# Row sums of squares of the next superblock's x, moved from the end of a superblock into its second merge

## The chip, the cores and the metric

The kernel runs on one core of a Trainium2 chip. The metric is the device time of one execution in microseconds; before the change three runs gave a median of 2172.32 us (2170.7 to 2173.43). PE, DVE, ACT, POOL and SP are the core's engines (matmul, vector, scalar, GpSimd, and the queue that issues most transfers). Each of them works through its instructions in the order in which they are laid out.

## What is computed

One layer over 2048 tokens of width 1024, in f32, with three branches that read the same normalised input `h`:

```
def rms_norm(x, g):
    y = xf * lax.rsqrt(jnp.mean(xf * xf, axis=-1, keepdims=True) + RMS_EPS)
    return (y * g.astype(jnp.float32)).astype(x.dtype)
...
h = rms_norm(x, norm_g[l])
p = h @ w_in[l]
...
y_a = rwkv7_mix(p_r, p_k, p_v, p_w, p_a, ...) * jax.nn.silu(z_a)
y_b = sliding_window_sink_attn(p_q, p_sk, p_sv, positions, ...) * jax.nn.silu(z_b)
y_c = memory_cross_attn(p_xq, mem, ...) * jax.nn.silu(z_c)
merged = (gates[:, :, 0] * (y_a @ w_proj_a[l]) + gates[:, :, 1] * (y_b @ w_proj_b[l])
          + gates[:, :, 2] * (y_c @ w_proj_c[l]))
x = x + (merged.astype(x.dtype) @ w_out[l]).astype(x.dtype)
```

The change concerns the mean of `xf * xf` over a token's 1024 values, of which `rms_norm` needs the inverse root.

## The kernel before

**Tiling.** The tokens are worked in four superblocks, 0 to 3, of 512 tokens. A projection is eight k-blocks of 128; each f32 operand is split into two parts (`hH`/`hL`, `yh`/`yl`, the two halves of `whl`), and three matmuls 128x512 (L505 to L507) make one k-block, so a merge step is 4 x 3 = 12 matmuls and a projection 24. Weights come in blocks through six `whl` buffers: in superblock 0 SP loads `raw`, ACT (L487) and DVE (L488) split it, and the parts are stored to DRAM; later superblocks load the parts ready made. Matmuls of projections and merges write two PSUM banks `mm` in turn; a bank is free again when its reader is done.

**A superblock.** Two streams of work are interleaved. One is the recurrent branch: preparation, an inverse by 31 dependent DVE steps on `Yi` and `ibc` (L863 to L865), its transpose (L868), 64 small matmuls that read it (L880), then the chain over chunks. The other is cross-attention, window attention in four pairs of heads (`swa_pair`, whose end L1253, `split_y` L1032 on ACT and L1033 on DVE makes a `yh`/`yl` tile), beside which runs the merge of branch c, then the merge of branch b (called the second merge here: eight steps, each with its gate projection, tanh L1261, and L1276/L1277), then the eight gates of branch a. After both streams come the rope tables (L566 to L587, with two sines on ACT that need another activation table), `x_scales` for the next superblock, the merge of branch a (third merge: L1276 empties a bank, L1277 adds, L1281 and L1283 split the sum), `x_cols` and `output`.

**x_scales and x_cols.** For the next 512 tokens, eight tiles 128x512 of x are loaded by transfers that ACT issues (L1318) into the ring `rt` of six buffers; ACT squares each (L1320) into a bf16 tile that nobody reads, of the ring `ibc` that the inverse uses too, and sums along the row by `accum_out`. DVE adds the two halves of a row (L1322), POOL takes the power -1/2 (L465, L467), DVE spreads the 512 scales (L543), four PE transposes (L545) turn them along the tokens, ACT copies them from PSUM (L1327). `x_cols` then loads eight tiles of transposed x (L1336), scales each (L1339) and splits it into `hH` and `hL` (L1341, L1342).

**What sets the order.** All instructions are collected in the order in which the program writes them, and a list scheduler (`lay_out`) with a table of costs lays out one order for each engine. It takes what is ready, by rank (the place in the program), and opens tiles of a ring in program order. A transfer is planned by it to land some 2.2 us after its issue plus its bytes. The ring `g2` has 11 buffers for the attention tiles, the gates and the output's tiles. Transfers report their landing on eight semaphores in turn, each of which is used again only when the transfer before on it has landed.

Of the kernel before, what the change touches and what calls it, by code (L numbers as in the profile page):

```python
# [9 lines left out]
F32 = mybir.dt.float32  # L10
F32R = mybir.dt.float32r
BF16 = mybir.dt.bfloat16
I32 = mybir.dt.int32
U8 = mybir.dt.uint8
AF = mybir.ActivationFunctionType
ALU = mybir.AluOpType
# [3 lines left out]
T, D, M = 2048, 1024, 256  # L20
TB = 512
# [12 lines left out]
EPS = 1e-6  # L34
# [282 lines left out]
def build(tc, A, nsb=4):  # L317
    nc = tc.nc
    es = ExitStack()
    V, S, G, PE = nc.vector, nc.scalar, nc.gpsimd, nc.tensor  # L320

    def pool(name, bufs, **kw):
        return es.enter_context(tc.tile_pool(name=name, bufs=bufs, **kw))
# [5 lines left out]
    rp = pool("rp", 1)  # L329
# [5 lines left out]
    xp = pool("xp", 1)  # L335

    def g2(dt=F32, shape=(128, TB)):
        return gp_.tile(list(shape), dt, name="g2")
# [3 lines left out]
    def mm_ps():  # L342
        return ps.tile([128, 512], F32, name="mm", bufs=2)
# [4 lines left out]
    def s_ps():  # L348
        return ps.tile([128, 512], F32, name="as_", bufs=2)
# [34 lines left out]
    memt, mem0, raws, x0, xt0 = [], [], [], [], []  # L384
# [75 lines left out]
    def rpow(out, in_, add, scale=1.0):  # L460

        if scale == 1.0:
            G.tensor_scalar(out, in_, add, None, op0=ALU.add)  # L463
        else:
            G.tensor_scalar(out, in_, scale, add, op0=ALU.mult, op1=ALU.add)  # L465
        n = out.shape[-1]
        G.tensor_tensor(out, out, mhalf[:, :n], op=ALU.pow)  # L467
# [12 lines left out]
    def wblock(src, key=None):  # L480
        w = wp.tile([128, 2, 512], F32R, name="whl")
        if key in kept:
            nc.sync.dma_start(w.bitcast(F32), kept[key])
            return w[:, 0], w[:, 1]
        raw = wp.tile([128, 512], F32, name="raw", bufs=RAW)
        nc.sync.dma_start(raw, src)
        S.activation(w[:, 0], raw, AF.Copy)  # L487
        V.tensor_tensor(w[:, 1], raw, w[:, 0].bitcast(F32), op=ALU.subtract)  # L488
        if key is not None and nsb > 1:
            kept[key] = dp.tile([128, 2, 512], F32, name=f"k{len(kept)}")  # L490
            nc.sync.dma_start(kept[key], w.bitcast(F32))
        return w[:, 0], w[:, 1]
# [8 lines left out]
    def gemm3(out, pairs):  # L501

        n = len(pairs)
        for i, ((lh, ll), (rh, rl)) in enumerate(pairs):
            PE.matmul(out, lh, rh, start=i == 0, stop=False)  # L505
            PE.matmul(out, lh, rl, start=False, stop=False)  # L506
            PE.matmul(out, ll, rh, start=False, stop=i == n - 1)  # L507
# [107 lines left out]
    def row_sums(rows):  # L615

        ss = xp.tile([128, 4, 2], F32, name="ss", bufs=2)
        for i, xr in enumerate(rows):
            sq = rp.tile([128, 512], BF16, name="ibc", bufs=2)
            if i % 2:  # L620
                V.tensor_tensor_reduce(sq, xr, xr, 1.0, 0.0, ALU.mult, ALU.add, ss[:, i // 2, 1:])
            else:
                S.activation(sq, xr, AF.Square, accum_out=ss[:, i // 2, :1])
        rs = xp.tile([128, 4], F32, name="rs", bufs=2)
        n = len(rows) // 2
        V.tensor_tensor(rs[:, :n], ss[:, :n, 0], ss[:, :n, 1], op=ALU.add)
        return rs
# [89 lines left out]
    def tmp(tag="rt", bufs=NRT):  # L717
        return rp.tile([128, TB], F32, name=tag, bufs=bufs)
# [539 lines left out]
    def gate(i, o, hT):  # L1258
        gp = proj(B_G + 8 * i + o, hT)
        t = gp_.tile([128, TB], F32, name="gt", bufs=2) if i else g2()  # L1260
        S.activation(t, gp, AF.Tanh, scale=0.5)  # L1261
        return t

    def merge(i, yh, yl, accs, hT, first=False, orange=range(8), gates=None):
        for o in orange:
            yield 3.718
            w = [t.rearrange("p (k c) -> p k c", k=4) for t in wblock(A["w_proj"][i, o], ("proj", i, o))]
            g = gates[o] if gates else gate(i, o, hT)
            pp = mm_ps()
            gemm3(pp, [((w[0][:, k], w[1][:, k]), (yh[k], yl[k])) for k in range(4)])  # L1270
            if first:
                acc = mp.tile([128, TB], F32, name="mB")
                V.scalar_tensor_tensor(acc, g, 1.0, pp, op0=ALU.add, op1=ALU.mult)
                accs.append(acc)
            else:
                V.scalar_tensor_tensor(g, g, 1.0, pp, op0=ALU.add, op1=ALU.mult)  # L1276
                V.tensor_tensor(accs[o], accs[o], g, op=ALU.add)  # L1277
# [25 lines left out]
    def masks():  # L1303
        full = g2()[:, :384]
        nc.sync.dma_start(full, A["gmask"])
        for i, t in enumerate((gmask, upto, over)):
            G.tensor_copy(t, full[:, i * 128:(i + 1) * 128])

    def x_scales(sb):

        if not sb:
            rs = row_sums(x0)
        else:
            ss = xp.tile([128, 4, 2], F32, name="ss", bufs=2)
            for i in range(4):
                for u in range(2):
                    xr = tmp()
                    nc.scalar.dma_start(xr, A["x"][sb * TB + i * 128:sb * TB + (i + 1) * 128, u * 512:(u + 1) * 512])  # L1318
                    sq = rp.tile([128, 512], BF16, name="ibc", bufs=2)
                    S.activation(sq, xr, AF.Square, accum_out=ss[:, i, u:u + 1])  # L1320
            rs = xp.tile([128, 4], F32, name="rs", bufs=2)
            V.tensor_tensor(rs, ss[:, :, 0], ss[:, :, 1], op=ALU.add)  # L1322
        rpow(rs, rs, EPS, 1.0 / D)
        bc = s_ps()
        bcast_T(bc, rs, 1, 4)
        rb = tmp()
        S.activation(rb, bc, AF.Copy)  # L1327
        return rb
# [19 lines left out]
    mv(3)  # L1348
    for i, _ in enumerate(mem_kv(mT, ms, mr)):
        if i == AT1:  # L1350
            rb = x_scales(0)
        if i == AT2:
            masks()
            hT = x_cols(0, rb)
    for sb in range(nsb):
        wa = proj(B_WA, hT)
        low = shift(wa, B_WA, pcol("mu_wa"), dcol("omu_wa"), sb, "rr_")
        S.activation(low[EV], low[EV], AF.Tanh)

        lwla = [rp.tile([128, TB], F32R, name=f"lwla{i}") for i in range(2)]  # L1360
        for t, h, o in zip(lwla, (EV, OD), (OD, EV)):
            S.activation(t[h], low[h], AF.Copy)
            V.tensor_tensor(t[o], low[h], t[h].bitcast(F32), op=ALU.subtract)
        yas = []
        ya, yb, yc_ = ([], []), ([], []), ([], [])
        accs = []

        def stream_r():
            parks = park(sb)
            dk = xp.tile([128, 4, NC_], F32, name="dk", bufs=1)  # L1370
            Pl = xp.tile([128, 4, NC_], F32, name="Pl", bufs=1)
            yts = []
            for p0 in (0, 2):
                group = []
                Nc = rp.tile([128, 2, NC_, 32], F32, name="Nc")
                for p in (p0, p0 + 1):
                    yield from rwkv_prep(p, p - p0, parks, dk, Pl, Nc, sb, hT, lwla, group)
                yield from rwkv_inverse(group, parks, Nc)
                yts += [g[2] for g in group]
            yield from rwkv_chain(parks, dk, Pl, hT, yts, yas)  # L1380
            yield 0.412

        def stream_f():
            for h in range(4):
                yield from cross_head(h, sb, hT, *yc_)
            if not sb:
                rope_tables(0)
            yield from swa_kv(sb, hT)
            yield 6.938
            for j in range(4):  # L1390
                yield from weave(swa_pair(j, sb, hT, *yb), merge(2, *yc_, accs, hT, first=True, orange=(2 * j, 2 * j + 1)))
            yield from merge(1, *yb, accs, hT)
            for o in range(8):
                gates.append(gate(0, o, hT))
                yield 5.908

        gates = []
        for _ in weave(*(paced(g, PACE[min(sb, 1)][i]) for i, g in enumerate((stream_r(), stream_f())))):
            pass
        for p in range(4):  # L1400
            split_y(yas[p], *ya, "a", p, sb)
        rb = None
        if sb + 1 < nsb:
            rope_tables(sb + 1)
            rb = x_scales(sb + 1)
        parts = []
        for o in range(8):
            for _ in merge(0, *ya, accs, hT, gates=gates, orange=(o,)):
                pass
            parts.append(split_acc(accs[o]))  # L1410
        if rb is not None:
            hT = x_cols(sb + 1, rb)
        output(sb, *zip(*parts))
# [92 lines left out]
```

## Time and profile before

| | us |
|---|---|
| median of three runs | 2172.32 |
| lowest, highest | 2170.7, 2173.43 |
| the profiled execution | 2170.66 |
| its span | 2168.9 |

A timeline row reads: start, duration, engine, line, operation, output<-input, shape, count, and in brackets how long the engine had been idle and what released it. Rows with a letter q behind the engine (ACTq) are that engine's queue issuing a transfer; that is not counted as busy time. Waits are listed as: who waited, for whom, total, times, longest. Buffer numbers are left out of names, and `g2` is written `g`.

### The profile page before, as it was taken

Reading aid. Unit: us, or ns where it says so; the run is one execution under the profiler, and the core shown is the slowest. Engines: PE = TensorE matmul, PEld = TensorE weight load, DVE = VectorE, ACT = ScalarE, POOL = GpSimd, SP = SyncE. Lnnn points to the kernel's source line nnn. Section 1 sums busy time; section 2 is a strip of 40 time slices with the busy share of each in tenths; the row PEclk is TensorE's granted clock in tenths of the full one; section 3 lists DMA queues with packets and bytes.
Section 4 is the critical chain, followed back from the end, with each engine's and each line's share of the span. In section 5 each row is a group of like instructions: output and inputs, shape, how many; then the busy total and the mean of one; then the engine's idle time right before and its main releaser. Section 6 shows DMA issues by size and latency. Waiting matters only on the chain.

```text
span 2168.9 us, 36206 instructions
## 1 busy us (share of the span) xinstructions
PE 2140.8 (99%) x13508; PEld 1768.5 (82%) x13508; DVE 1546.6 (71%) x3683; ACT 818.7 (38%) x1741; POOL 135.4 (6%) x159
## 2 busy tenths in 40 slices
PE   8999999999999999999999999999999999999998
PEld 6888788887788888888888888888878888888887
DVE  8799999567478889655537988954455798894432
ACT  6665554245244343303414444411523434431220
POOL 2001000010001000001000000000100010000100
PEclk9999999999999999999999999999999999999999
DMA  9987787979966476575776656676676566658556
GB/s 339 323 278 264 254 272 257 346 265 316 339 203 207 164 220 214 197 262 193 265 255 202 205 186 195 207 260 195 232 258 232 194 194 206 210 170 290 171 192 203
DMA packets 254751, 511.79 MB, mean 236 GB/s; under 512 B 38256, under 2 KB 120432, under 8 KB 254576
## 3 DMA queue, kind: packets, MB, share of 16 engines
q1 hardware_dynamic: 238448, 480.12, 66.1%
q10 hardware_dynamic: 16128, 29.37, 4.0%
q8 instruction: 107, 1.75, 0.3%
q14 instruction: 68, 0.56, 0.1%
HBM read 375.71 MB, written 133.69 MB: 235 GB/s over the span
## 4 chain that ended last, share of the span: by engine, by line
PE 88%; DMA 7%; DVE 3%; ACT 1%; issue 1%; SPq 0%; ACTq 0%; POOL 0%; DVEq 0%; POOLq 0%
PE mm L507 22%; PE mm L506 22%; PE mm L505 22%; PE oo L1245 1%; PE rw L983 1%; PE mm L1295 1%; DMA rt<-in_x 1%; PE rw L966 1%; DMA g<-in_x 1%; PE mm L1294 1%; PE mm L1293 1%; PE rw L806 1%; DMA out<-g 1%; PE rw L826 1%; PE oo L806 1%
## 5 line engine op out<-in xcount | busy, mean ns | idle before, releaser
L505 PE MATMUL mm<-hH,whl 128*128 128x512 f32 x1888 | 744.6, 395 | 4.6 <-DVE g L1019 4.3
L506 PE MATMUL mm<-hL,whl 128*128 128x512 f32 x1888 | 744.1, 394 | 0.8 <-DVE hL L1342 0.8
L507 PE MATMUL mm<-hH,whl 128*128 128x512 f32 x1888 | 744.3, 394 | 0.0
L505 PEld LDWEIGHTS mm<-hH,whl 128*128 128x128 f32 x1888 | 354.7, 188 | 76.1 <-DVE g L1019 4.5
L507 PEld LDWEIGHTS mm<-hH,whl 128*128 128x128 f32 x1888 | 355.0, 188 | 71.7 <-issue 1.2
L506 PEld LDWEIGHTS mm<-hL,whl 128*128 128x128 f32 x1888 | 355.1, 188 | 71.6 <-DVE hL L1342 1.6
L487 ACT ACTIVATE whl<-raw 128x512 fp32r<-128x512 f32 x162 | 101.5, 629 | 159.2 <-PE mm L507 97.7
L505 PE MATMUL mm<-yh,whl 128*128 128x512 f32 x384 | 150.4, 392 | 1.5 <-ACT g L1261 1.5
L506 PE MATMUL mm<-yl,whl 128*128 128x512 f32 x384 | 150.5, 392 | 0.0
L507 PE MATMUL mm<-yh,whl 128*128 128x512 f32 x384 | 150.3, 392 | 0.0
L488 DVE TENSOR_TENSOR whl<-raw,whl 128x512 fp32r<-128x512 f32 x162 | 111.3, 689 | 34.8 <-ACT whl L487 33.0
L863 DVE STREAM_SHUFFLE ibc<-Nc 128x496 f32<-128x496 f32 (+30 forms) x248 | 114.4, 473 | 0.1
L864 DVE TENSOR_TENSOR ibc<-ibc,Yi 128x496 f32<-128x496 f32 (+30 forms) x248 | 104.6, 422 | 4.2
L1261 ACT ACTIVATE gt<-mm 128x512 f32<-128x512 f32 x64 | 38.0, 594 | 179.1 <-PE mm L507 179.0
L865 DVE TENSOR_TENSOR Yi<-Yi,ibc 128x496 f32<-128x496 f32 (+30 forms) x248 | 103.4, 417 | 1.1
L505 PEld LDWEIGHTS mm<-yh,whl 128*128 128x128 f32 x384 | 72.1, 188 | 16.5 <-ACT g L1261 1.9
L506 PEld LDWEIGHTS mm<-yl,whl 128*128 128x128 f32 x384 | 72.1, 188 | 14.9
L507 PEld LDWEIGHTS mm<-yh,whl 128*128 128x128 f32 x384 | 72.1, 188 | 14.8 <-issue 0.2
L1300 DVE SCALAR_TENSOR_TENSOR g<-mm,g 128x512 f32<-128x512 f32 x16 | 11.0, 690 | 88.8 <-PE mm L1295 88.8
L463 POOL TENSOR_SCALAR st<-st 128x4 f32<-128x4 f32 (+1 forms) x32 | 11.9, 371 | 964.8 <-DVE st L1060 471.4
L1218 ACT ACTIVATE g<-g,mxs,st 128x128 f32<-128x128 f32 x128 | 61.5, 484 | 24.9 <-DVE mxs L1211 24.9
L1276 DVE SCALAR_TENSOR_TENSOR gt<-gt,mm 128x512 f32<-128x512 f32 x32 | 21.9, 685 | 58.5 <-PE mm L507 58.3
(1829 smaller groups left out, 3623.3 us busy)
## 6 DMA issues: line engine op xcount, KB each, us to landing
whl<-k SPq DMA_DIRECT2D x486, 512.0 KB, 3.5
k<-whl SPq DMA_DIRECT2D x162, 512.0 KB, 4.8
raw<-in_w_in SPq DMA_DIRECT2D x118, 256.0 KB, 3.8
fq<-big SPq DMA_DIRECT2D x64, 256.0 KB, 4.3
fb<-big SPq DMA_DIRECT2D x64, 256.0 KB, 4.5
big<-fq SPq DMA_DIRECT2D x32, 512.0 KB, 6.8
big<-fb SPq DMA_DIRECT2D x32, 512.0 KB, 5.9
g<-in_x ACTq DMA_DIRECT2D x32, 256.0 KB, 4.8
```

Of the source, the lines that this page charges most:

```text
L487: S.activation(w[:, 0], raw, AF.Copy)
L488: V.tensor_tensor(w[:, 1], raw, w[:, 0].bitcast(F32), op=ALU.subtract)
L505: PE.matmul(out, lh, rh, start=i == 0, stop=False)
L506: PE.matmul(out, lh, rl, start=False, stop=False)
L507: PE.matmul(out, ll, rh, start=False, stop=i == n - 1)
L806: m = PE.matmul(g[:, c], BK[h, c0 + c], Q[h, c0 + c], start=True, stop=True)
L863: V.stream_shuffle(bc[:, :, :w], N_[:, :, s + 1:], [s] * 32)
L864: V.tensor_tensor(bc[:, :, :w], bc[:, :, :w], Y[:, :, s:s + 1].to_broadcast([128, n, w]), op=ALU.mult)
L865: V.tensor_tensor(Y[:, :, s + 1:], Y[:, :, s + 1:], bc[:, :, :w], op=ALU.add)
L1218: S.activation(P_, P_, AF.Exp, scale=r2[:, b, i:i + 1], bias=mx[:, b, i:i + 1], accum_out=mx[:, b, 2 + i:3 + i])
L1261: S.activation(t, gp, AF.Tanh, scale=0.5)
L1276: V.scalar_tensor_tensor(g, g, 1.0, pp, op0=ALU.add, op1=ALU.mult)
```

## The change

`x_scales` is cut in two. `x_sums(sb)` is a generator that loads the eight x tiles, one at each `yield`, now into the ring `g2`, and squares each in place; it ends with the addition and the power. It is stepped in the second merge, once behind each of the eight merge steps, in superblocks 0 to 2, for the superblock that follows. `x_scales(rs)` keeps the rest and stays where it was. For superblock 0 itself the calls are the same as before.

```
-    def x_scales(sb):
-        if not sb:
-            rs = row_sums(x0)
-        else:
...
-                    xr = tmp()
-                    nc.scalar.dma_start(xr, A["x"][...])
-                    sq = rp.tile([128, 512], BF16, name="ibc", bufs=2)
-                    S.activation(sq, xr, AF.Square, accum_out=ss[:, i, u:u + 1])
+    def x_sums(sb):
+        ss = xp.tile([128, 4, 2], F32, name="ss", bufs=2)
+        for i in range(4):
+            for u in range(2):
+                xr = g2()
+                nc.scalar.dma_start(xr, A["x"][...])
+                S.activation(xr, xr, AF.Square, accum_out=ss[:, i, u:u + 1])
+                yield
+        rs = xp.tile([128, 4], F32, name="rs", bufs=2)
+        V.tensor_tensor(rs, ss[:, :, 0], ss[:, :, 1], op=ALU.add)
         rpow(rs, rs, EPS, 1.0 / D)
+        yield rs
+    def x_scales(rs):
         bc = s_ps()
...
-            yield from merge(1, *yb, accs, hT)
+            ahead = x_sums(sb + 1) if sb + 1 < nsb else iter(())
+            for o in range(8):
+                yield from merge(1, *yb, accs, hT, orange=(o,))
+                next(ahead, None)
+            scales.append(next(ahead, None))
...
-            rb = x_scales(sb + 1)
+            rb = x_scales(scales[-1])
```

In the changed kernel the load is L1315, the square L1316, the addition L1319; L1327, L1336, L1339, L1341 and L1342 become L1328, L1337, L1340, L1342 and L1343. The text goes by the old numbers of those that exist in both.

ACT in superblock 1, around the end of the last window attention pair, before (L1234 copies its transposed weights, L1032 splits its result, L1261 is a gate's tanh of the second merge, L873 takes up the finished inverse):

```order
L1018 ACTIVATE g_9554<-mm 128x512
L1234 ACTIVATE g_9564<-as__9559 128x512
L1234 ACTIVATE g_9575<-as__9570 128x512
L1032 ACTIVATE yh<-g_9554 128x512
L1261 ACTIVATE gt<-mm 128x512
L873 ACTIVATE big<-Yi 32x8x32 x8
```

and after, at the same place:

```order
L1234 ACTIVATE g_9567<-as__9562 128x512
L1315 DMA g_9855<-in_x 128x512
...
L1315 DMA g_10464<-in_x 128x512
L1316 ACTIVATE g_9855,ss<-g_9855 128x512
L1315 DMA g_10515<-in_x 128x512
L1316 ACTIVATE g_9964,ss<-g_9964 128x512
L1032 ACTIVATE yh<-g_9546 128x512
L1316 ACTIVATE g_10073,ss<-g_10073 128x512
L1261 ACTIVATE gt<-mm 128x512
L1316 ACTIVATE g_10202,ss<-g_10202 128x512
```

All eight loads and the first two squares now stand ahead of L1032, the other six behind it. Superblock 2 has the same order. In superblock 0 all eight loads and one square stand ahead of L1032; there the seventh and eighth load reuse the landing semaphores of the first and second.

DVE in superblock 0, from the last operation of the rope tables (L587) into the third merge, before (L488 splits a weight block):

```order
L587 TENSOR_SCALAR cosT<-rt 128x512
L1276 SCALAR_TENSOR_TENSOR g_5195<-g_5195,mm 128x512
L1277 TENSOR_TENSOR mB<-mB,g_5195 128x512
L488 TENSOR_TENSOR whl<-raw,whl 128x512
L1276 SCALAR_TENSOR_TENSOR g_5369<-g_5369,mm 128x512
L488 TENSOR_TENSOR whl<-raw,whl 128x512
L1283 TENSOR_TENSOR mB<-mB,g_5907 128x512
L1277 TENSOR_TENSOR mB<-mB,g_5369 128x512
L1276 SCALAR_TENSOR_TENSOR g_5530<-g_5530,mm 128x512
```

and after:

```order
L587 TENSOR_SCALAR cosT<-rt 128x512
L1276 SCALAR_TENSOR_TENSOR g_5224<-g_5224,mm 128x512
L488 TENSOR_TENSOR whl<-raw,whl 128x512
L1277 TENSOR_TENSOR mB<-mB,g_5224 128x512
L1276 SCALAR_TENSOR_TENSOR g_5398<-g_5398,mm 128x512
L1283 TENSOR_TENSOR mB<-mB,g_5899 128x512
L488 TENSOR_TENSOR whl<-raw,whl 128x512
L1277 TENSOR_TENSOR mB<-mB,g_5398 128x512
L1340 TENSOR_TENSOR rt<-rt 128x512
L1276 SCALAR_TENSOR_TENSOR g_5559<-g_5559,mm 128x512
```

The scaling of transposed x (L1340, formerly L1339) has come in ahead of the third L1276; before, it began behind the sixth. In superblocks 1 and 2 two of them stand ahead of the second L1276.

PE at the same end of superblock 0, before, where L545 are the four transposes of the scales:

```order
L505 MATMUL mm<-yh,whl 128x512
L506 MATMUL mm<-yl,whl 128x512
L545 MATMUL as__5876<-c_ident,rt 128x128 x4
L507 MATMUL mm<-yh,whl 128x512
L505 MATMUL mm<-yh,whl 128x512
```

and after:

```order
L506 MATMUL mm<-hL,whl 128x512
L507 MATMUL mm<-hH,whl 128x512
L545 MATMUL as__5868<-c_ident,rt 128x128 x4
L505 MATMUL mm<-yh,whl 128x512
L506 MATMUL mm<-yl,whl 128x512
```

They have moved from inside the third merge to the row ahead of its first matmul, right behind the last gate's projection.

More of the change, by code (lines that the diff above doesn't have):

```diff
@@ L1307, in masks @@
             G.tensor_copy(t, full[:, i * 128:(i + 1) * 128])
-    def x_scales(sb):
-        if not sb:
-            rs = row_sums(x0)
-        else:
-            ss = xp.tile([128, 4, 2], F32, name="ss", bufs=2)
-            for i in range(4):
-                for u in range(2):
-                    xr = tmp()
-                    nc.scalar.dma_start(xr, A["x"][sb * TB + i * 128:sb * TB + (i + 1) * 128, u * 512:(u + 1) * 512])
-                    sq = rp.tile([128, 512], BF16, name="ibc", bufs=2)
-                    S.activation(sq, xr, AF.Square, accum_out=ss[:, i, u:u + 1])
-            rs = xp.tile([128, 4], F32, name="rs", bufs=2)
-            V.tensor_tensor(rs, ss[:, :, 0], ss[:, :, 1], op=ALU.add)
+    def x_sums(sb):
[3 more added lines that the diff above has]
+                xr = g2()
+                nc.scalar.dma_start(xr, A["x"][sb * TB + i * 128:sb * TB + (i + 1) * 128, u * 512:(u + 1) * 512])
+                S.activation(xr, xr, AF.Square, accum_out=ss[:, i, u:u + 1])
+                yield
+        rs = xp.tile([128, 4], F32, name="rs", bufs=2)
+        V.tensor_tensor(rs, ss[:, :, 0], ss[:, :, 1], op=ALU.add)
         rpow(rs, rs, EPS, 1.0 / D)
+        yield rs
+    def x_scales(rs):
         bc = s_ps()
@@ L1350, in build @@
         if i == AT1:
-            rb = x_scales(0)
+            rs = row_sums(x0)
+            rpow(rs, rs, EPS, 1.0 / D)
+            rb = x_scales(rs)
         if i == AT2:
@@ L1395, in stream_f @@
                 yield 5.908
-        gates = []
+        gates, scales = [], []
         for _ in weave(*(paced(g, PACE[min(sb, 1)][i]) for i, g in enumerate((stream_r(), stream_f())))):
```

## The prediction

> **What bounds the kernel now.** I read the page first, then busy time by stretch, then what the PE waited for.
>
> ```profile
> span 2168.9 us, 36206 instructions
> PE 2140.8 (99%) x13508; PEld 1768.5 (82%) x13508; DVE 1546.6 (71%) x3683; ACT 818.7 (38%) x1741; POOL 135.4 (6%) x159
> 340.00:380.00 40.00, 40.00 (x214) 32.73 (x214) 39.52 (x132) 19.29 (x46) 0.00 (x0) 1.00 0.76 252
> 500.00:540.00 40.00, 36.79 (x164) 29.89 (x163) 31.66 (x54) 23.15 (x46) 2.55 (x3) 1.00 0.95 318
> 880.00:900.00 20.00, 20.00 (x175) 16.37 (x174) 17.12 (x71) 6.51 (x14) 0.00 (x0) 1.00 0.45 152
> 1406.00:1426.00 20.00, 20.00 (x175) 16.37 (x174) 17.79 (x74) 6.39 (x16) 0.00 (x0) 1.00 0.47 158
> ```
>
> The PE is busy 99% of the span, at full granted clock (1.00) in these stretches, and the change takes no matmul away. So it can win only PE idle time, and any new PE idle time is lost one to one. The second stretch is the end of superblock 0, where the squares stand now; the other three are where they go. The last three columns are clock, DMA share and GB/s, the pairs are busy time and instructions of PE, weight load, DVE, ACT and POOL. At the end the DMA share is 0.95 and the PE loses 3.2 us of 40; in the new places the PE loses nothing, and DVE is busy 99%, 86% and 89% of the time.
>
> The PE's waits, by line waited for (total, times, longest):
>
> ```profile
> PE as__5876 L545 <- DVE rt L543: 1.7, 1, 1.7
> PE mm L505 <- ACT g L1261: 1.5, 1, 1.5
> PE as__16206 L545 <- DVE rt L543: 0.6, 1, 0.6
> ```
>
> L543 copies the row scales that the four transposes of L545 broadcast: 1.7 us at the end of superblock 0, 0.6 at that of superblock 2, nothing at that of 1. The 1.5 us is the wait for a matmul bank that the last gate's tanh (L1261) must empty. These three, 3.8 us or 0.18% of the time, are all that the change can reach.
>
> **What it removes.** The transposes now stand ahead of the third merge and their input depends on sums made over 100 us earlier: 1.7 + 0.6 = **2.3 us** go. What is late next there is the scaled x itself, which no matmul needs before the next superblock. The 1.5 us I follow through ACT's timeline at the end of superblock 0, with the DVE row that feeds it:
>
> ```profile
> 508.20 0.58 ACT L1261 ACTIVATE g<-mm 128x512 f32<-128x512 f32 x1
> 510.86 0.33 ACTq L1318 DMA_DIRECT2D rt<-in_x  x1
> 511.22 1.28 ACT L583 ACT_TABLE_LOAD   x1 [1.58 <-DMA raw<-in_w_proj]
> 513.57 0.62 ACT L1320 ACTIVATE ibc<-rt 128x512 bf16<-128x512 f32 x1
> 514.19 0.62 ACT L585 ACTIVATE rt<-rt 128x512 f32<-128x512 f32 x1
> 515.34 1.28 ACT L1261 ACT_TABLE_LOAD   x1
> 516.64 0.60 ACT L1261 ACTIVATE g<-mm 128x512 f32<-128x512 f32 x1
> 509.51 0.42 DVE L582 TENSOR_SCALAR rt<-rt 128x512 f32<-128x512 f32 x1
> 515.40 0.39 PE L507 MATMUL mm<-yh,whl 128*128 128x512 f32 x1
> 517.29 0.50 PE L505 MATMUL mm<-yh,whl 128*128 128x512 f32 x1 [1.50 <-ACT g L1261]
> 530.42 0.83 DVE L543 COPY rt<-rs 128x512 f32<-128x512 f32 x1
> ```
>
> An x load at 510.86 had to wait for a weight transfer and held ACT 1.58 us; behind it stood the sine's table load, one square (0.62) on the way, the second table load and the tanh. Without load and square the tanh could come 2.2 us earlier; L543 now stands ahead of L582 and takes its 0.83 of that back. Of the wait of 1.5 **1.4 us** go. Together 3.7 us.
>
> **What it adds.** Eight loads and eight squares for each of three superblocks, as many as before, on the same queue; the squares write in place instead of to bf16. Prices:
>
> ```profile
> L1320 ACT ACTIVATE ibc<-rt x24: 613/622/633, 508.9 to 1571.2; 128x512 bf16<-128x512 f32 x24
> L1318 ACTq DMA_DIRECT2D rt<-in_x x24: 334/356/1010, 502.4 to 1565.0; - x24
> DMA to landing us min/median/max: 3.6/5.3/7.9
> rt<-in_x ACTq DMA_DIRECT2D x8, 256.0 KB, 6.7
> rt<-in_x ACTq DMA_DIRECT2D x5, 256.0 KB, 4.6
> DMA to landing us min/median/max: 3.5/5.0/8.1
> L487 ACT ACTIVATE whl<-raw 128x512 fp32r<-128x512 f32 x162 | 101.5, 629 | 159.2 <-PE mm L507 97.7
> L488 DVE TENSOR_TENSOR whl<-raw,whl 128x512 fp32r<-128x512 f32 x162 | 111.3, 689 | 34.8 <-ACT whl L487 33.0
> ```
>
> A square takes 0.62 us, a load 0.36 to issue. The third row is the landing time of the 24 x loads, the fourth their median from 500 to 530 us, the fifth that from 1020 to 1032, the sixth is that of the loads of the transposed x (L1336). ACT has room for 8 x 0.98 = 7.8 us in each new place (it is idle half of the first and two thirds of the others), and the weight splits behind it mostly wait for the PE to give a buffer back (97.7 of their 159.2 us of idle time), so they run ahead of it by what six buffers hold, 5 x 2.7 us. So neither is a cost; a hold of ACT of more than some 10 us would make it one. SP's row of transfers is the same before and after; POOL's two small steps on the sums move ahead of others, and POOL is 6% busy. The f32 write in place is unknown in this trace: the nearest row, a 128x512 f32 ACTIVATE of 0.60 to 0.63, says nothing lost or gained; at most it is +-0.05 on work that is hidden.
>
> What costs is order. ACT runs in order, and the first squares stand **ahead of L1032**, the split of the last attention pair that merge and DVE wait for. Superblock 1:
>
> ```profile
> 883.08 0.60 ACT L1234 ACTIVATE g<-as__9570 128x512 f32<-128x512 f32 x1
> 888.57 0.63 ACT L1032 ACTIVATE yh<-g 128x512 fp32r<-128x512 f32 x1 [4.89 <-DVE g L1253]
> 889.41 0.69 DVE L1033 TENSOR_TENSOR yl<-g,yh 128x512 fp32r<-128x512 f32 x1
> 891.36 0.39 PE L505 MATMUL mm<-yh,whl 128*128 128x512 f32 x1
> 895.51 0.71 DVE L868 STREAM_TRANSPOSE ibc<-Yi 128x512 f32<-128x512 f32 x1
> 896.66 1.20 PE L880 MATMUL rw<-ibc,big 32*32 32x32 f32 x64
> ```
>
> The loads go out from 883.7. At 4.6 us (the DMA share here is 0.45) the first lands at 888.3; two squares of 0.62; L1032 starts at 889.5 instead of 888.57, 0.9 late. The PE's use of yh at 891.36 still has room. But DVE, full with the inverse's steps, stands at L1033 until yh is there, so L868 ends 0.9 later, and another 0.16 for the rs addition that now stands in that row: 897.3 for 896.22. The PE's 64 small matmuls at 896.66 then wait: **0.7 us**. Superblock 2 has the same order: **0.7**.
>
> Superblock 0 has one square ahead of L1032, but the eighth load must first wait for the landing of the second:
>
> ```profile
> 355.51 0.60 ACT L1234 ACTIVATE g<-as__4107 128x512 f32<-128x512 f32 x1
> 360.68 0.63 ACT L1032 ACTIVATE yh<-g 128x512 fp32r<-128x512 f32 x1 [2.18 <-DVE g L1253]
> 361.78 0.39 PE L505 MATMUL mm<-yh,whl 128*128 128x512 f32 x1
> 362.01 0.39 PE L505 MATMUL mm<-hH,whl 128*128 128x512 f32 x1
> ```
>
> Second load at 356.5, landed at 361.8 by the overall median of 5.3 (the share is 0.76, between the two stretches), eighth load issued by 362.2, square until 362.8, yh at 363.4. The PE wants it two matmuls (0.23 each, the last two rows) later than before, at 362.2: **1.3 us** with the signal.
>
> At the ends, the scaling of x now runs inside the third merge, and DVE has L1340, which waits for a load of transposed x, ahead of the L1276 that empties a bank. Superblock 0: issue about 515.7, landed 5.0 later at 520.7; ACT's fifth such load waits for that, then its split for L1283; that split ends at 521.7, and five DVE operations of 0.69 (L488's mean; 0.6 where they overlap), the last of them L1276, end at 524.9. The PE has three blocks of 12 matmuls, 8.2 us, from 515.6 and wants the bank at 523.8: **1.1 us**. In superblocks 1 and 2 no split and no such wait stand in between; the same count ends within 0.2 us of the need: 0.1 each.
>
> Sum: -3.7 + 1.3 + 0.7 + 0.7 + 1.1 + 0.2 = **+0.3 us**. The profiled execution took 2170.66 us (span 2168.9), so 2171.0 for one like it; it lies 1.7 below the median of the three runs, 2172.32, against which I predict **2172.6**.
>
> [...] The change issues early as seen from the scales, but lets ACT wait for the landing at once, ahead of work that others need; that is the added wait above.
>
> **The rivals.**
>
> *Loads land sooner* in the emptier stages, at the least of the rows, 3.6 us. Then L1032 is on time everywhere (0.9 - 1.0, 1.3 - 1.7) and L1340 too: only the gain is left, -3.7, 2168.6. For it: shares of 0.45 and 0.47. Against: eight loads in a row share the queue, and the five from 1020 on had 4.6. [...]
>
> *Loads land late*, the slower one: L1032 held behind squares in each of the three stages, at the 6.7 us of the burst from 500 on: superblock 0 +2.7, superblocks 1 and 2 +2.8 each, with 1.3 at the ends less 3.7: +5.9, 2178.2. It gets past 0.2% (4.3 us) when landing averages over 6.2 us in the three places. For it: that burst was as deep; against: the share there was 0.95.
>
> *The change does not do what it says*: the PE's waits at the ends only change their name, tanh or L1276 in place of L543, and nothing waits in the middle: between -1 and +1, 2172.3.
>
> **Chances.** Forecast 0.62, early landing 0.16, late landing 0.12, no effect 0.10. 0.2% is 4.3 us, about what a measurement of this kernel can tell from no change. Of early landing, 0.04 pass -0.2%, where one more wait of the PE goes with it; of late landing, 0.10 pass it; 0.01 of the forecast on either side. Faster 0.05, same 0.84, slower 0.11. The range takes in both ends: 2168.6 to 2178.
>
> **What will show it.** Right: no L545 wait on L543 among the PE's waits; the tanh wait of 1.5 gone or under 0.3; L1032 starting 0.5 to 1.5 us later after L1234 in superblocks 1 and 2, with a PE wait ahead of L880; a PE wait of 1 to 2 us on yh near 362; x loads there landing in 4 to 6 us. Wrong, if L880 comes no later, if the yh wait is over 3 us, or if a new wait on L1276 at the ends is larger than what L545 lost.

## The result and the profile after

Six runs of the changed kernel have a median of 2181.23 us (2178.92 to 2184.13), six of the kernel before 2172.88 (2168.81 to 2174.93): ratio 1.0038, 95% interval 1.0027 to 1.0049. It is slower by some 8 us; the forecast was 2172.6 and no change, with a range up to 2178.0, so the time lies above the range, and a loss came where none was forecast. The profiled execution took 2184.13 us, the slowest of the six: its span is 13.5 us longer than that of the profile before, where the medians differ by 8.35.

The head of the page after:

```profile
span 2182.3 us, 36193 instructions
PE 2149.0 (98%) x13508; PEld 1775.3 (81%) x13508; DVE 1545.1 (71%) x3683; ACT 813.5 (37%) x1737; POOL 134.5 (6%) x159
```

The PE runs as many matmuls as before, but is busy 8.2 us longer. So matmuls took longer, beside what was waited. The three rows of its waits that matter most here, each new or larger than before:

```profile
PE mm L505 <- ACT yh L1032: 6.4, 2, 3.7
PE as__6302 L1293 <- DVE g L1300: 2.8, 1, 2.8
PE rw L880 <- DVE ibc L868: 0.9, 1, 0.9
```

L545 behind L543 and the tanh are gone from the list at the ends of superblocks 0 and 2. In their place stand two waits on `yh` (3.7 us in superblock 0, 2.7 in superblock 2), one at L880 in superblock 1, and a longer one on L1300, which empties the output's banks. (Three new waits on L1276 are of 0.4 us at most.) What follows the first of them is seen by stretches (the last three columns are clock, DMA share and GB/s):

```profile
362.00:366.25 4.25, 2.00 (x9) 1.32 (x7) 1.55 (x7) 0.00 (x0) 0.00 (x0) 1.00 1.04 403
366.25:373.10 6.85, 5.38 (x13) 4.24 (x14) 4.37 (x13) 5.65 (x16) 0.00 (x0) 0.50 0.51 190
373.10:376.50 3.40, 3.40 (x17) 2.76 (x16) 3.06 (x11) 2.08 (x6) 0.00 (x0) 1.00 0.92 262
1431.20:1434.60 3.40, 3.40 (x10) 2.63 (x9) 3.30 (x20) 2.52 (x9) 0.00 (x0) 0.50 0.51 159
```

After the wait the granted clock is 0.50 for 6.8 us: 13 matmuls in 5.4 us of work, where the third row has 17 in 3.4. Half of those 5.4 us, 2.7, are lost on top of the 3.7 that were waited. The last row is the stretch behind the `yh` wait of superblock 2: 3.4 us at half clock, so 1.7 are lost there.

The same points of the program in the two profiled executions show where the time went (start of the instruction named, in us):

| point | before | after | later by | in this stage |
|---|---|---|---|---|
| superblock 0, second group's first transposes (L842) | 270.19 | 271.84 | 1.65 | +1.65 |
| superblock 0, second group's L880 | 379.78 | 387.92 | 8.14 | **+6.5** |
| superblock 0, first matmul of the output (L1293) | 538.85 | 543.72 | 4.87 | **-3.3** |
| superblock 1, first L842 | 642.57 | 650.58 | 8.01 | **+3.1** |
| superblock 1, second group's L880 | 896.66 | 905.68 | 9.02 | +1.0 |
| superblock 1, output | 1066.52 | 1074.83 | 8.31 | -0.7 |
| superblock 2, first L842 | 1169.27 | 1178.01 | 8.74 | +0.4 |
| superblock 2, second group's L880 | 1423.32 | 1437.15 | 13.83 | **+5.1** |
| superblock 2, output | 1593.31 | 1606.43 | 13.12 | -0.7 |
| superblock 3, first L842 | 1695.80 | 1710.21 | 14.41 | +1.3 |
| end of the span | 2168.87 | 2182.34 | 13.47 | -0.9 |

The first row lies ahead of the change; it is the start and a half-clock stretch near 264, which lasted 3.4 us before and 6.8 after, behind the same wait of 4.3. The third merge gave back 3.3 us at the end of superblock 0, as counted on. The stages that hold the second merge lost 12.6 in the three superblocks together.

Now the held instruction itself. ACT at the end of the window attention of superblock 2, before:

```profile
1409.73 0.60 ACT L1234 ACTIVATE g<-as__14675 128x512 f32<-128x512 f32 x1
1415.23 0.63 ACT L1032 ACTIVATE yh<-g 128x512 fp32r<-128x512 f32 x1 [4.89 <-DVE g L1253]
```

and after, with the PE's row that waits for it and the landing time of the weight block that SP sent out at 1420.07:

```profile
1418.45 0.60 ACT L1234 ACTIVATE g<-as__14659 128x512 f32<-128x512 f32 x1
1418.46 3.73 ACTq L1315 DMA_DIRECT2D g<-in_x  x7
1422.23 0.63 ACT L1316 ACTIVATE g<-g 128x512 f32<-128x512 f32 x1 [3.18 <-DMA g<-in_x]
1427.66 0.34 ACTq L1315 DMA_DIRECT2D g<-in_x  x1
1428.32 0.63 ACT L1316 ACTIVATE g<-g 128x512 f32<-128x512 f32 x1 [5.36 <-DMA whl<-k]
1428.95 0.61 ACT L1032 ACTIVATE yh<-g 128x512 fp32r<-128x512 f32 x1
1429.61 0.50 PE L505 MATMUL mm<-yh,whl 128*128 128x512 f32 x1 [2.68 <-ACT yh L1032]
whl<-k SPq DMA_DIRECT2D x1, 512.0 KB, 7.5
```

From the last L1234 to L1032 it was 5.5 us, and is 10.5. Seven loads go out in 3.7 us and the first square follows. Then ACT stands still for 5.4 us until the **eighth load** can be issued: it reuses the landing semaphore (103 in the trace) of the weight block sent out at 1420.07, which needs 7.5 us beside the x loads (3.5 was the median of the 486 such blocks before). Only then come the second square and L1032. Without a load in this stage (squares alone, below) the block at this place lands after 3.2 us:

```profile
whl<-k SPq DMA_DIRECT2D x1, 512.0 KB, 3.2
```

In the nine bursts of this kernel and of two runs below (squares behind, loads without squares) the eighth load went out 0.1 us after a landing: in superblock 0 that of the second x load, in the others that of such a weight block. That fits the semaphore and not some buffer. What stands still in the trace is all of ACT: from 1422.96 to 1427.66 it has no instruction, and its next one comes after 5.36 us of idle time.

### The profile page after: what moved, and what is told of

Read it like the earlier page. It is cut to its first block, busy times and chain, and to the rows that moved or that the text cites. A ratio compares the mean times of both kernels' runs of the same rounds, so it can differ in the third digit from the quotient of the medians.

```text
span 2182.3 us, 36193 instructions
## 1 busy us (share of the span) xinstructions
PE 2149.0 (98%) x13508; PEld 1775.3 (81%) x13508; DVE 1545.1 (71%) x3683; ACT 813.5 (37%) x1737; POOL 134.5 (6%) x159
## 4 chain that ended last, share of the span: by engine, by line
PE 87%; DVE 6%; DMA 5%; issue 1%; ACT 1%; SPq 0%; POOL 0%; ACTq 0%; DVEq 0%; POOLq 0%
PE mm L507 22%; PE mm L506 22%; PE mm L505 22%; DMA g<-in_x 1%; PE rw L983 1%; PE oo L1245 1%; PE mm L1295 1%; PE mm L1293 1%; PE rw L966 1%; PE mm L1294 1%; PE rw L806 1%; DMA out<-g 1%; PE rw L826 1%; DVE mB L1277 1%; DMA k<-whl 1%
## 5 line engine op out<-in xcount | busy, mean ns | idle before, releaser
L488 DVE TENSOR_TENSOR whl<-raw,whl 128x512 fp32r<-128x512 f32 x162 | 111.3, 689 | 35.3 <-ACT whl L487 33.3
L1261 ACT ACTIVATE gt<-mm 128x512 f32<-128x512 f32 x64 | 37.9, 593 | 177.7 <-PE mm L507 177.6
L1300 DVE SCALAR_TENSOR_TENSOR g<-mm,g 128x512 f32<-128x512 f32 x16 | 11.0, 690 | 92.0 <-PE mm L1295 92.0
L1276 DVE SCALAR_TENSOR_TENSOR gt<-gt,mm 128x512 f32<-128x512 f32 x32 | 21.9, 685 | 59.5 <-PE mm L507 59.3
```

## Experiments

The theory: **ACT is held by the issue of its own loads**, each of which must wait for an earlier transfer on its semaphore; L1032 stands behind them. Rivals: the squares that wait for their x hold it (the prediction's step); the traffic of 2 MB more in this stage; ACT's own time; the new ring or the order at the ends.

Each kernel is compared with runs of the kernel before on the same chip, of median 2171.67 (first four kernels), 2171.6 (next four) and 2171.85 (last two); the three groups ran on different chips, so kernels of different groups are set against each other by their distance from these medians.

**Squares behind L1032, loads left ahead**

```
-                S.activation(xr, xr, AF.Square, accum_out=...)
+                behind(S.activation(xr, xr, AF.Square, accum_out=...), split["b", 3])
```

`behind(a, b)` makes the scheduler put `a` behind `b`; `split["b", 3]` is the L1032 of the last pair.

> Changed kernel, but each square is ordered behind the split L1032 of the last pair; the eight loads stay ahead of it. Before: 2172.9 us, changed: 2181.2. If the squares that wait for their x hold L1032 (the step of the prediction): L1032 is on time, the waits on yh (3.7 and 2.7 us) go under 1, and the time is 2171 to 2174. If it is the issue of the loads, each waiting for an earlier transfer to land (the eighth load of superblock 2 was issued 9.2 us after the first), the squares are worth only the 0.6 to 1.3 us that they ran ahead of L1032: the waits stay over 1.5 and the time is 2178 to 2181. If it is the traffic of the loads itself, nothing changes: 2181.

2178.45 us, 1.0025 (1.0016 to 1.0034). ACT in superblock 2 (L1317 are the loads, L1033 is the split, L1236 was L1234):

```profile
1414.75 0.60 ACT L1236 ACTIVATE g<-as__14659 128x512 f32<-128x512 f32 x1
1414.75 8.83 ACTq L1317 DMA_DIRECT2D g<-in_x  x8
1423.63 0.63 ACT L1033 ACTIVATE yh<-g 128x512 fp32r<-128x512 f32 x1 [8.28 <-DMA g<-in_x]
```

No square is ahead of the split any more, and it is still 8.9 us behind L1236: the eight loads take 8.8 us to issue. The waits on `yh` are 2.2 and 1.1 us, those at L880 sum to 1.7. The loss is 6.78 us, where the changed kernel's was 8.35, and the intervals of the two ratios overlap. So the squares are the smaller part, if they count at all, and the issue is the larger one.

**Loads and squares behind L1032**

```
-                nc.scalar.dma_start(xr, A["x"][...])
+                behind(nc.scalar.dma_start(xr, A["x"][...]), split["b", 3])
                 S.activation(xr, xr, AF.Square, accum_out=...)
```

> Changed kernel, but loads and squares are ordered behind L1032 of the last pair; same stage, same ring, same traffic some 5 us later. If ACT's order is the cause (either the squares or the issue of the loads), the waits on yh and the half clock behind them go, unless a tanh or a weight split behind the squares is held in its place: 2169 to 2175. If the traffic of 2 MB in this stage is the cause, weight blocks are late as before and the time stays at 2179 to 2182. If the ends of the superblocks are the cause (output of superblock 0 lost 3 us), it stays at 2176 or more.

2170.34 us, 0.9994 (0.9985 to 1.0003). No wait of the PE on `yh` or at L880 is left in the second merges, with the same loads in the same stage. So traffic as such is not the cause. The loss is gone; a gain that could be measured is not there either. That is taken up below.

**Neither loads nor squares**

```
+        G.memset(ss, 512.0)
-                xr = g2()
-                nc.scalar.dma_start(xr, A["x"][...])
-                S.activation(xr, xr, AF.Square, accum_out=...)
```

> The loads and squares of the later superblocks are left out, the sums are a constant. If only the new place costs and the ends gain what was forecast (3.7 us), this is the bound: 2168.5 to 2170, with no yh wait, no wait on L543 and no tanh wait at the ends. If the new order at the ends costs as much as it gains (output loads, x columns), it is 2171 to 2174 with long waits on L1300 or L1276.

The sums are a constant here. 2168.75 us, 0.9986 (0.9977 to 0.9996), within the bound's range. But the output of superblock 0 has a wait on L1300 of 2.8 us, as in the changed kernel, and here there is neither load nor square. So that wait comes from the earlier third merge, not from the new stage.

**The old place, the new ring**

```
-            ahead = x_sums(sb + 1) if sb + 1 < nsb else iter(())
-            for o in range(8):
-                yield from merge(1, *yb, accs, hT, orange=(o,))
-                next(ahead, None)
-            scales.append(next(ahead, None))
+            yield from merge(1, *yb, accs, hT)
...
-            rb = x_scales(scales[-1])
+            rb = x_scales(list(x_sums(sb + 1))[-1])
```

> Loads and squares back at the end of the superblock, but in place in the ring g2 as in the changed kernel. If the ring is neutral: 2171.5 to 2174 with the old waits on L543 and on a tanh. If buffers of g2 taken at the end delay the output's tiles or the gates, slower: 2175 to 2180, with longer waits on L1300. If ring rt was what held the end up, faster: under 2171.

2170.41 us, 0.9993 (0.9984 to 1.0002). The time lies in the range of the third answer (under 2171), but the interval takes in no change, so a gain by the ring is not shown. The waits on L543 are back (1.8 and 0.5 us). The ring and the write in place cost nothing that can be measured.

**Loads without squares**

```
+        G.memset(ss, 512.0)
-                S.activation(xr, xr, AF.Square, accum_out=...)
```

> Changed kernel with the loads where they are, the squares left out and the sums a constant. If the issue of the loads holds ACT (each waits for an earlier transfer's landing), the yh waits and the half clock stay as with the squares ordered behind: 2176 to 2179.5, with the eighth load of superblock 2 issued over 5 us after the seventh. If it is the squares, L1032 is on time and the time is that without loads and squares: 2168 to 2171.

2175.81 us, 1.0019 (1.0010 to 1.0028): 0.2 below the range of the first answer, clear of the second. With no square in this stage, superblock 2 shows the same hold (L1316 is the load here):

```profile
1415.82 5.56 ACTq L1316 DMA_DIRECT2D g<-in_x  x2
1421.42 0.63 ACT L1032 ACTIVATE yh<-g 128x512 fp32r<-128x512 f32 x1 [8.40 <-DMA g<-in_x]
```

The seventh and eighth load take 5.56 us to issue, where two take 0.7 otherwise. The loss is 4.2 us, against 6.8 with the squares behind; the intervals overlap. One difference is that in superblock 0 the list put the split ahead of the eighth load, and no `yh` wait is left in that superblock. In superblock 1 the weight block took 6.8 us to land in this run, and the PE waited 1.1 us on `yh` there.

**Squares without loads**

```
-    def x_sums(sb):
+    def x_sums(sb, hT):
...
-                nc.scalar.dma_start(xr, A["x"][...])
-                S.activation(xr, xr, AF.Square, accum_out=...)
+                S.activation(xr, hT[0][:, 2 * i + u].bitcast(F32), AF.Square, accum_out=...)
```

> Changed kernel without the loads: the squares take a resident tile, eight of 0.62 us, in the same place (six to eight of them ahead of L1032). The sums are then not those of x. If waiting for transfers is all of the cost, L1032 comes less than 1 us late and the time is 2168 to 2171.5. If ACT's own time for the squares counts, there are yh waits of 1.5 us or more in superblock 0 and L880 waits: 2174 to 2179.

The squares read `hT`, which lies on the chip. 2171.69 us, 0.9995 (0.9986 to 1.0004); 0.2 over the first range. Six squares (superblock 0) or eight stand ahead of L1032 and no wait on `yh` is left, so ACT has the room for the squares themselves.

**Only the eighth load behind L1032**, and the squares

```
-                nc.scalar.dma_start(xr, A["x"][...])
-                S.activation(xr, xr, AF.Square, accum_out=...)
+                load = nc.scalar.dma_start(xr, A["x"][...])
+                if i == 3 and u == 1:
+                    behind(load, split["b", 3])
+                behind(S.activation(xr, xr, AF.Square, accum_out=...), split["b", 3])
```

> Seven loads ahead of L1032, the eighth load and all squares behind it. With the squares behind alone: 2178.5. If the hold is that of the last load, which takes up again a landing signal that a weight transfer of this very stretch still owes, superblocks 1 and 2 lose nothing (L1032 within 1 us of its need, no wait over 0.5), superblock 0 keeps under 1.5 us: 2170.5 to 2174. If the burst of loads holds ACT wherever it is cut: 2176 to 2179.

2173.11 us, 1.0004 (0.9995 to 1.0013). Superblock 2:

```profile
1413.13 3.73 ACTq L1317 DMA_DIRECT2D g<-in_x  x7
1418.59 0.63 ACT L1033 ACTIVATE yh<-g 128x512 fp32r<-128x512 f32 x1 [4.86 <-DVE g L1255]
1422.88 0.33 ACTq L1317 DMA_DIRECT2D g<-in_x  x1
```

The split starts when DVE hands it its input, after 4.86 us of idle time, as in the kernel before (4.89). The eighth load is as late as ever, and nobody waits for it. One transfer's place in ACT's row is worth 5.3 us (a loss of 6.8 with the squares alone behind, of 1.5 here). In superblock 0, where the sixth load waits too, 0.8 us on `yh` remain.

**A place one stage later**, between the gates of branch a

```
+            yield from merge(1, *yb, accs, hT)
             ahead = x_sums(sb + 1) if sb + 1 < nsb else iter(())
-            for o in range(8):
-                yield from merge(1, *yb, accs, hT, orange=(o,))
-                next(ahead, None)
-            scales.append(next(ahead, None))
             for o in range(8):
                 gates.append(gate(0, o, hT))
                 yield 5.908
+                next(ahead, None)
+            scales.append(next(ahead, None))
```

> A third place: a load and a square behind each of the eight gates of branch a, one stage later; ring and ends as in the changed kernel. The loads then go out one at a time, some 5 us apart, but each square still waits on ACT for its own landing (about 5 us), with a gate's tanh or a split of ya behind it. If such a hold matters only where the PE wants the held result within 5 us, the tanh has the other bank's time of 5.4 us: 2169 to 2172. If it matters everywhere: waits on a tanh or on yh of 1 us and more, 2174 to 2180.

2172.13 us, 1.0001 (0.9992 to 1.0010), 0.1 over the first range: no difference. Loads go out one at a time, and no wait on a tanh or on `yh` stands out. So where nothing urgent stood behind it, the hold cost nothing that can be measured.

**Where the gain went: the output's fourth tile in another ring.** In the output, ACT loads four x tiles per half into `g2`, where the eight split sums leave room for three; the fourth load waits for the first store to land. This is the run with loads and squares behind (L1302 was L1300, L1303 the store, L1301 the load, L1295 was L1293):

```profile
556.33 0.68 DVE L1302 SCALAR_TENSOR_TENSOR g<-mm,g 128x512 f32<-128x512 f32 x1
557.05 1.52 ACTq L1303 DMA_DIRECT2D out<-g  x2
562.58 3.02 ACTq L1301 DMA_DIRECT2D g<-in_x  x3
567.79 0.69 DVE L1302 SCALAR_TENSOR_TENSOR g<-as__6130,g 128x512 f32<-128x512 f32 x1 [7.70 <-DMA g<-in_x]
568.54 0.50 PE L1295 MATMUL as__6302<-whl,g 128*128 128x512 f32 x1 [2.19 <-DVE g L1302]
569.20:572.60 3.40, 3.40 (x10) 2.63 (x9) 1.39 (x2) 1.26 (x2) 0.00 (x0) 0.50 0.32 116
```

Store and load take 11.5 us here from the first bank's L1302 to the fourth's (11.0 in the kernel before, 12.1 in the changed one), so an earlier merge does not shorten them; the PE then waits 2.19 us and runs 3.4 us at half clock. The edit, on the kernel with loads and squares behind and on the kernel before:

```
-                xr = g2()
+                xr = g2() if tt < 3 else tmp()
```

> Loads and squares behind L1032 as before (2170.3), and in the output the fourth x tile of each half goes into the ring rt in place of g2, so that its load no longer waits for the first store to land. In the kernel with loads and squares behind, the third merge of superblock 0 came 3.4 us earlier and the wait on L1300 that follows (2.2 us, with half clock for 3.4) took most of it back. If that chain of store and load is where the gain went, the wait and the half clock go: 2164 to 2167.5. If the PE then waits for the next thing (x columns, weights), 2168.5 to 2171.

> The kernel before with the same edit of the output and nothing else. Its waits on L1300 in the profile sum to 5 us (0.6, 0.9, 0.9, 0.6, 1.8), with no half clock. If they go: 2167 to 2170, and the version with early sums is 2 to 4 us faster than this one, the gain of the third merge that the prediction counted. If the difference between the two is under 1 us, that gain is lost elsewhere too.

2164.36 us with early sums, 0.9966 (0.9954 to 0.9978): **7.5 us faster than before**. On the kernel before, 2168.42, 0.9986 (0.9977 to 0.9995). The difference is 4.1 us, a shade over the expected 2 to 4. So the sums made early are worth that much, once the chain behind them is cut. The PE's waits from 500 to 545 us in the kernel before with that edit, and one stretch after them:

```profile
PE as__5876 L545 <- DVE rt L543: 1.9, 1, 1.9
PE mm L505 <- ACT g L1261: 0.8, 1, 0.8
532.70:536.10 3.40, 3.40 (x11) 2.83 (x12) 2.24 (x4) 1.50 (x3) 0.00 (x0) 0.50 0.74 216
```

Here the old wait on L543 itself is followed by half clock. With early sums there is no wait at that place, and none on L1302 over 0.6 us at the output.

## Why the prediction was wrong

- **What it removes** held. The waits on L543 and on the tanh went, and superblock 0 gained 3.3 us in its third merge against 1.7 + 1.4 counted; superblock 2 gained 0.7 against 0.6.
- **L1340 at the end of superblock 0, 1.1 us**, did not come: the PE has no wait from 500 to 545 us. The first load of transposed x went out at 522.00, 2.6 us ahead of the second merge step (524.57), where the forecast had both at one time (515.7 and 515.6). So the third L1276 ended at 532.18, and the PE used that bank from 532.73 on.
- **Superblocks 1 and 2, 0.7 each: the step that failed.** "At 4.6 us (the DMA share here is 0.45) the first lands at 888.3; two squares of 0.62; L1032 starts at 889.5 instead of 888.57, 0.9 late." It let ACT wait for the landing of an x tile. It left out that the eighth load, which stands between the two squares, waits for its semaphore as well, and that the transfer it waits for is a weight block that is late in this very burst (7.5 us, where it takes 3.2 without the loads). Such a hold was worked out for superblock 0 alone, though the prediction had read one off its own row as well: the x load at 510.86 that waited for a weight transfer and held ACT 1.58 us. Measured: 5.1 us in superblock 2. In superblock 1, 1.0: there the weight block had landed after 4.4 us. That this is near the 0.7 is luck: with the loads alone the same block took 6.8.
- **Superblock 0, 1.3 us**: right in kind, wrong in size. "Second load at 356.5, landed at 361.8 by the overall median of 5.3": the loads of this burst landed after 5.3, 7.2 and 9.1 us (least, median, most), the second after 8.3; and the sixth load was held too, by a weight transfer that took 5.7. ACT issued the last three loads from 363.01 on, over 3.4 us. The wait on `yh` was 3.7 us, past the 3 that the prediction had set as a sign of being wrong.
- **The clock** was in no term of the sum. Each wait was priced at its own length. The 3.7 us in superblock 0 brought 6.8 us at half clock, and the 2.7 us of superblock 2 brought 3.4: 2.7 and 1.7 us more (half of the busy time in them).
- **What is late next.** "What is late next there is the scaled x itself, which no matmul needs before the next superblock." Next was L1300 and the chain of store and load in front of it. It took back most of the 3.3 us in superblock 0: 1.5 us more of waiting (3.1 for 1.6), and 1.7 by half clock.

The forecast's rival of late landing (2178.2) had the sign and nearly the size. Its condition was an average landing over 6.2 us: the three bursts had medians of 7.2, 5.3 and 6.4, so it was about met. But of its mechanism, L1032 held by squares, the run with the squares behind shows 1.6 us (8.35 less 6.78), which is not clear of noise; what cost most was the issue. That its time came near was luck.

That the x loads make the weight block late is shown: in superblock 2 it took 6.8, 6.9 and 6.3 us in three other runs with seven or eight of them ahead of the split, and 3.2 with none. How far that is owed to sharing, and how far to the order in which the queues are served, was not tried.

## What to carry to other kernels

Here a transfer that ACT issued waited for an earlier landing on its semaphore, and all that stood behind it on ACT waited too (5.4 us in superblock 2), so list for each transfer what its issue waits for, not only who waits for its data. Put early loads behind the urgent instruction of the stage, and look for a burst's last transfers, which here came round to semaphores still owed (the eighth load of eight). A gain ahead of a chain of fixed length (the output's store and load, 11.0 to 12.1 us here) only moves the wait to that chain: price the next wait, cut it as well, and only then is the gain seen.

## What the runs showed of the hardware

A PE wait of some 2 us or more mostly cost more than its length here. In the profiles before and after, past the first 60 us and ahead of their end, each wait of 2.68 us and over (2.68, 2.81, 3.72, 4.25 and 4.27) was followed by half clock, for 3.41 or 6.83 us, and none of 1.8 or less. In two experiments half clock for 3.4 us shows behind waits of 1.9 (the kernel before with the output's edit) and 2.19 (loads and squares behind). A wait of 1.93 that ended at 20.02 us in the profile before brought none. In the clock record of the profile after, the four stretches at half clock last 3.413 or 6.827 us; their starts, 263.85, 366.24, 577.87 and 1431.20 us, lie 30, 62 and 250 times 3.413 us apart, and the last begins 1.6 us after the PE had gone on (1429.61). At half clock a matmul of 128x512 starts every 0.43 us instead of 0.23:

```profile
368.74 0.63 PE L505 MATMUL mm<-hH,whl 128*128 128x512 f32 x1
369.17 0.63 PE L506 MATMUL mm<-hL,whl 128*128 128x512 f32 x1
```

The same wait of 4.3 us near 261 us brought 3.4 us of half clock before and 6.8 after. It ended at

```profile
264.65 0.69 PE L505 MATMUL mm<-hH,whl 128*128 128x512 f32 x1 [4.27 <-DVE g L1019]
265.42 0.79 PE L505 MATMUL mm<-hH,whl 128*128 128x512 f32 x1 [4.25 <-DVE g L1019]
```

so the profile after was 0.8 us behind; at the L842 of the table's first row it was 1.65 behind. By an estimate the longer stretch cost 0.9 us more: it began at 263.85, while the PE still waited, so of its 6.83 us 5.25 fell on work, and half of that is lost, against half of 3.41. Such differences may be a small part of why runs of one kernel lie up to 8 us apart.
